# Two attentions of a two-block decoder layer: the values' product taken by turns of two heads, and the chunk mask moved out of TensorE

## The chip, the cores and the metric

One core of a Trainium2 chip runs the whole kernel. The metric is the device time of one execution in microseconds (us); a program of one core has one span, that of its engines from the first instruction to the last. The engines are TensorE (PE in the profile, its weight loads PEld), VectorE (DVE), ScalarE (ACT), GpSimd (POOL) and SyncE (SP), which issues the DMAs.

## The reference

Two blocks follow each other on a sequence of 1024 positions and 1024 features. The first block runs a gated delta rule and a stick-breaking attention beside each other and merges them. The second runs two softmax attentions, MLA and a differential one, then a feed-forward part. Three attentions are concerned here; cut down to them the reference is:

```python
# stick-breaking: 8 heads of 64, causal, blocks of 128 queries
a = where(mask, exp(log_sigmoid(z) + rest), 0)          # z = q k^T * scale, rest: a reversed cumulative sum
o = einsum('bhqk,bhkd->bhqd', a, v)
# MLA: 8 heads, keys of 96 features, values of 64
allowed = (k_idx // 64) <= (q_idx // 64)
probs = softmax(where(allowed, q k^T * scale, -1e30))
o = einsum('bhqk,bhkd->bhqd', probs, v)
# differential: 4 heads, two maps each, bias from a table by distance
logits = where(allowed, q k^T * scale + bias, -1e30)
attn = softmax(logits[0]) - lam * softmax(logits[1])
o = einsum('bhqk,bhkd->bhqd', attn, v)
```

`allowed` is the chunk mask: a query sees all keys of its own chunk of 64 and of the chunks before. Within a tile of 128 queries (two chunks) that hides the tile's second chunk of keys from the tile's first 64 queries.

## The kernel before, in words

All matrix products are float32. An input of a large product is split into a high and a low part, and `mm3` (L250 to L254) multiplies high by high, high by low and low by high. The attention's other products (transposes, the values' product) are plain float32.

**Order of the work.** The kernel is written for one core in a framework that takes the instructions in program order as priorities, plans them against one another, and gives each engine its own order from that; each engine then runs its order strictly. So a product that is written later can stand between two that are written earlier, where the plan saw the second wait. `attend` (L782) drives an attention over a list of items: at step n it calls `s0` of item n (scores and softmax) and `s1` of item n-2 (transpose and values' product), with a `yield` after each. At a `yield`, `mix` steps a second generator, the fill: independent projections, in proportion to the items done. Stick-breaking (`sb`, L823) has the gate projections as fill, with a pool of two PSUM banks for them and one bank (`PT`) for transposes; `mla` (L1169) has the rest of `diff_proj`, and after it the next stage's `out2a`; `diff` has `out2a` and `ple_proj`. `mla_proj`, the stage before `mla`, has five and three banks and most of `diff_proj` as its fill.

**Items.** `pairs` (L885) lists four pairs of heads (p), each over eight tiles of 128 queries (i). For i below 4 an item holds both heads of the pair; from i = 4 on each head is an item of its own. A head at tile i has i + 1 blocks of 128 keys.

**Values' product, before.** `attend_pv` (L889) transposes up to four blocks of an item into the one `pt` bank (L903), copies them to `aT` (L904), does so again for the next four, and then multiplies all blocks, first head first (L907): the weights are 128 x 64 values, so head 0 writes rows 0 to 63 of `po` and head 1 rows 64 to 127. In the trace each float32 product is two records. A transpose uses all 128 columns of the array, the values' product 64.

**Chunk mask, before.** In `mla` and in `diff` a fourth product, in bfloat16, adds -1e30 to the last 64 keys of the last block (L1201, L1304), with the constant `negch`; it closes the group of products of each score tile.

**Around them.** `mla` reads its queries and keys from DRAM (`dr_mla`, 96 feature rows, high and low part; L1171), to which `mla_proj` wrote them with `l_st` (L1127). `diff` loads for each head a `strip` of bias (L1276) that `L1307` adds to the scores while it takes their maximum. `qk_stack` (L719) writes the differential queries and keys to DRAM through tiles `qb_st`, two buffers, evacuated by ACT (L301) and DVE (L302), two tiles behind each other for each half.

Of the kernel before, what the change touches and what calls it, by code (L numbers as in the profile page):

```python
# [75 lines left out]
    return np.ascontiguousarray(onehot), np.ascontiguousarray(rope.reshape(8, 128, 2, 32).transpose(1, 0, 2, 3))  # L76


def layout(inputs):
    a = {k: np.asarray(v) for k, v in inputs.items()}  # L80
    o = {}
# [49 lines left out]
    o["lam"] = np.ascontiguousarray(np.stack([a[f"lambda_{n}_2"][0] for n in ("q1", "k1", "q2", "k2")]))  # L131
    o["rel"] = np.ascontiguousarray(a["rel_bias_2"])
    o["onehot"], o["rope"] = _tables()
    return o


# [15 lines left out]
class Kern:  # L152
# [38 lines left out]
    def consts(self):  # L191
        nc, d, const = self.nc, self.d, self.const
        self.vec = {}
        self.later = []

        def load(n, shape, src):
            t = const.tile(shape, F32, name=n)
            self.vec[n] = t
            return lambda: nc.sync.dma_start(t, src)
        for n in ("b_gate", "cw1", "g_dn", "g_ql", "g_kvl", "g_do", "cw2", "cb2"):  # L200
            self.later.append(load(n, list(d[n].shape), d[n]))
        for n, w in (("a_log", 4), ("dt_bias", 4), ("g_sq", 64), ("g_sk", 64), ("g_dq", 64), ("g_dk", 64), ("g_mq", 96), ("g_mk", 96)):
# [12 lines left out]

        self.negch = const.tile([128, 64], BF16, name="negch")
        nc.gpsimd.memset(self.negch, 0.0)
        nc.gpsimd.memset(self.negch[0:64, :], NEG)
        self.ones = const.tile([128, 128], F32, name="ones")
        nc.gpsimd.memset(self.ones, 1.0)  # L220

        def casts():
            nc.vector.tensor_copy(self.identb, self.ident)
            nc.vector.tensor_copy(self.negub, negu)
        self.later.append(casts)
# [491 lines left out]
    def qk_stack(self, pool, xn, ws, gains, dst):  # L717
# [23 lines left out]
        def stack(gi, half, raw):  # L741
            for pr in range(2):
                p = 2 * (gi % 2) + pr
                st = pool.tile([128, 2, 512], F32R, tag="qb_st", name="qb_st", bufs=2)
                pt = self.PT()
                for j in range(4):
                    nc.tensor.transpose(pt[:, j, :], raw[:, j, pr * 128:pr * 128 + 128], self.ident)
                self.split_evac(st[:, 0], st[:, 1], pt.rearrange("p a b -> p (a b)"))
                a = 2 * (gi // 2)
                nc.sync.dma_start(dst[p, :, a:a + 2, half * 512:half * 512 + 512], st.bitcast(F32))  # L750
                yield
# [70 lines left out]
    def sb(self):  # L822
# [14 lines left out]
        def s0(p, i, hs):  # L837
# [28 lines left out]
            cs = new("cs", 4)  # L866
# [4 lines left out]
            st[p, i, hs] = cs  # L871

        def s1(p, i, hs):
            cs = st.pop((p, i, hs))
            qk, v, ob = st[p]
            po = self.attend_pv(sp, po_, st, cs, v, i, hs, nc.vector.tensor_copy, nc.vector.tensor_copy)
            if hs[-1] == 1:
                nc.vector.tensor_copy(ob[:, i * 128:i * 128 + 128], po)
                if i == NT - 1:
                    nc.sync.dma_start(self.dr_oa[1, :, p, :], ob)  # L880

        yield from self.attend(self.pairs(), s0, s1)
        es.close()
# [2 lines left out]

        return [(p, i, hs) for p in range(4) for i in range(NT) for hs in ([(0, 1)] if i < 4 else [(0,), (1,)])]

    def attend_pv(self, sp, po_, st, e, v, i, hs, *copy):  # L889

        nc = self.nc
        mm = nc.tensor.matmul
        if hs[0] == 0:
            st["po"] = po_.tile([128, 128], F32, tag="po", name="po")
        po = st["po"]
        blocks = [(a, j) for a in range(len(hs)) for j in range(i + 1)]
        aT = sp.tile([128, 8, 128], F32, tag="aT", name="aT", bufs=2)
        step = 4 if i != 2 else 3
        for b0 in range(0, len(blocks), step):
            pt = self.PT()  # L900
            bs = blocks[b0:b0 + step]
            for b, (a, j) in enumerate(bs):
                nc.tensor.transpose(pt[:, b, :], e[:, a, j * 128:j * 128 + 128], self.ident)  # L903
            copy[b0 > 0](aT[:, b0:b0 + len(bs), :], pt[:, :len(bs), :])  # L904
        for b, (a, j) in enumerate(blocks):
            h = hs[a]
            mm(po[64 * h:64 * h + 64, :], v[:, j, h * 64:h * 64 + 64], aT[:, b, :], start=j == 0, stop=j == i)  # L907
        return po

    def merge_in(self):  # L910
# [78 lines left out]
    def layer2(self):  # L989
        nc, d, tc, vec = self.nc, self.d, self.tc, self.vec  # L990
        dr = lambda n, s: self.dram.tile(s, F32, name=n)
        self.dr_mla = dr("dr_mla", [8, 96, 4, 1024])
        self.dr_mv = dr("dr_mv", [128, NT, 512])
        self.dr_dqk = dr("dr_dqk", [4, 128, 4, 1024])
        self.dr_dv = dr("dr_dv", [128, NT, 512])
# [27 lines left out]

    def mla_proj(self):
        nc, d, tc, vec, lp = self.nc, self.d, self.tc, self.vec, self.lp
        rope = lp.tile([128, NT, 2, 32], F32, name="rope")
        nc.sync.dma_start(rope, d["rope"])
        qlT = [self.pair(lp, f"qlT{h}", 2) for h in range(2)]
# [90 lines left out]
        def fin(raw, hg, half, part):  # L1119

            for h in range(4):
# [5 lines left out]
                nc.sync.dma_start(self.dr_mla[4 * hg + h, :, part:part + 2, half * 512:half * 512 + 512], st.bitcast(F32))  # L1127

        units = []
        w = {}  # L1130
# [27 lines left out]

    def mla(self):
        nc, d, tc = self.nc, self.d, self.tc  # L1160
        mm = nc.tensor.matmul
# [5 lines left out]

        def load(p, hh, c, half):

            t = sp.tile([96, 2, 512], F32R, tag=f"qk{c}{half}{hh}", name="qk", bufs=1 + (hh == 1 and c == 1 and half == 0))  # L1170
# [10 lines left out]
        def s0(p, i, hs):  # L1181
# [10 lines left out]
            for a, h in enumerate(hs):  # L1192
                qk = st[p][0]
                qt = qk[h, 0, i // 4]
                for c0 in range(0, nk, 512):
                    n = min(512, nk - c0)
                    last = c0 + n == nk
                    kt = qk[h, 1, c0 // 512]
                    self.mm3(z[:, a, c0:c0 + n], [qt[:, 0, q], qt[:, 1, q]], [kt[:, 0, :n], kt[:, 1, :n]], True, not last)
                    if last:  # L1200
                        mm(z[:, a, nk - 64:nk], self.identb, self.negch, start=False, stop=True)  # L1201
            zz = z[:, :, :nk]
            nm, s, r = (self.small.tile([128, 2], F32, tag=f"a_{n}", name=f"a_{n}", bufs=4)[:, :len(hs)] for n in "msr")
            nc.vector.reduce_max(nm, zz, axis=AX.X, negate=True)
            e = sp.tile([128, 1024], F32, tag="e", name="e", bufs=3)[:, :len(hs) * nk].rearrange("p (a k) -> p a k", a=len(hs))
# [5 lines left out]
            st[p, i, hs] = e  # L1211

        def s1(p, i, hs):
            e = st.pop((p, i, hs))
            qks, v = st[p]
            po = self.attend_pv(sp, po_, st, e, v, i, hs, nc.scalar.copy, nc.vector.tensor_copy)
            if hs[-1] == 1:
                if i % 4 == 0:
                    st["ob"] = sp.tile([128, 512], F32, tag="ob", name="ob", bufs=1)
                nc.vector.tensor_copy(st["ob"][:, i % 4 * 128:i % 4 * 128 + 128], po)  # L1220
                if i % 4 == 3:
                    nc.sync.dma_start(self.dr_mix[:, p, (i - 3) * 128:(i + 1) * 128], st["ob"])

        yield from self.attend(self.pairs(), s0, s1)
        es.close()
# [13 lines left out]
    def diff(self):  # L1239
# [30 lines left out]
        def first(hd):  # L1270
# [3 lines left out]
            skew = self.dr_f[hd][0:1, 127:128]  # L1274
            strip[hd] = qp.tile([128, 1024], F32, tag="strip", name="strip", bufs=2)
            nc.sync.dma_start(strip[hd], bass.AP(tensor=skew.tensor, offset=skew.offset, ap=[[1152, 128], [1, 1024]]))  # L1276
            st[hd] = qk, v, o, sp.tile([128, NT], F32, tag="o_ss", name="o_ss", bufs=2)

        def s0(hd, i):
# [13 lines left out]
            for m in range(2):  # L1293
# [2 lines left out]
                z = zs[:, m if i < 4 else 0]  # L1296
                for c0 in range(0, nk, 512):
                    n = min(512, nk - c0)
                    last = c0 + n == nk
                    kt = qk[c0 // 512][1]  # L1300
                    mm(z[:, c0:c0 + n], qt[:, 0, m, q], kt[:, m, :n], start=True, stop=False)
                    mm(z[:, c0:c0 + n], qt[:, 1, m, q], kt[:, m, :n], start=False, stop=not last)
                    if last:
                        mm(z[:, nk - 64:nk], self.identb, self.negch, start=False, stop=True)  # L1304
                e = sp.tile([128, 1024], F32, tag=f"e{m}", name="e", bufs=(3, 2)[m])[:, :nk]
                mx = self.small.tile([128, 1], F32, tag="a_nm", name="a_nm", bufs=4)
                nc.vector.tensor_tensor_reduce(e, z[:, :nk], strip[hd][:, 896 - 128 * i:1024], 1.0, -3.0e38, ALU.add, ALU.max, mx)  # L1307
# [367 lines left out]
```

## Time and profile before

| | |
|---|---|
| runs shown | 2704.09, 2707.13, 2709.62 us; median 2707.13 us |
| profiled execution | 2711.15 us, of which the span is 2709.3 us |
| busy share of the span | PE 94%, PEld 80%, DVE 54%, ACT 32%, POOL 39% |
| mean granted clock of TensorE | 0.982 |

The profile shows one execution. The profiled execution's own time is 1.85 us longer than its span and 4.0 us over the median of the runs shown. Busy times of an engine are unions of its instructions; matmuls are pipelined, so what a product costs is read from the start of one to the start of the next.

### The profile page before, as it was taken

The page shows a single profiled execution, that of the slowest core. Times are in us where ns is not written, and L with a number is a line of the kernel's source. Part 1 is how long each engine was busy: PE and PEld are TensorE (multiplying, and loading weights), DVE is VectorE, ACT ScalarE, POOL GpSimd, SP SyncE. Part 2 cuts the span into 40 slices and gives each one's busy share as a digit, 9 for nine tenths or more (in the row PEclk, how much of TensorE's full clock was granted, in tenths as well). Part 3 has the DMA queues.
Part 4 walks back from the last instruction along what each step waited for, and adds up shares of the span by engine and source line. Part 5 has one row for each costly group of instructions (what it writes and reads, how often), then busy time and mean ns, then how long its engine had stood idle before and what let it go on. Part 6 is the DMA issues. An engine that isn't in the chain of part 4 may idle for free.

```text
span 2709.3 us, 38990 instructions
## 1 busy us (share of the span) xinstructions
PE 2548.5 (94%) x15298; PEld 2173.9 (80%) x15298; DVE 1461.3 (54%) x2837; ACT 864.7 (32%) x1575; POOL 1057.1 (39%) x920
## 2 busy tenths in 40 slices
PE   6998999999999989999889998889999999999999
PEld 6888888877777768989777787788777777777789
DVE  6565565275666554457844336666454454534372
ACT  3322222154444342122324335463333333201031
POOL 2533332122122234544533232223677777634322
PEclk9999999999999999999989999999999999999999
DMA  4433223153421355322674337554122222523222
GB/s 155 132 103 107 79 86 101 56 142 97 119 86 63 133 175 190 105 82 82 207 200 128 94 123 171 170 186 156 55 79 70 86 85 64 196 83 109 70 82 90
DMA packets 152335, 311.46 MB, mean 115 GB/s; under 512 B 14132, under 2 KB 57396, under 8 KB 152152
## 3 DMA queue, kind: packets, MB, share of 16 engines
q1 hardware_dynamic: 152152, 308.97, 36.7%
q8 instruction: 121, 1.98, 0.3%
q14 instruction: 62, 0.51, 0.1%
HBM read 211.91 MB, written 99.37 MB: 115 GB/s over the span
## 4 chain that ended last, share of the span: by engine, by line
PE 61%; DVE 10%; DMA 5%; ACT 3%; issue 2%; POOL 1%; SPq 0%; ACTq 0%; DVEq 0%; POOLq 0%
PE pj L1525 15%; PE pj L254 10%; PE pj L253 10%; PE pj L252 10%; PE po L907 5%; PE pt L903 3%; DMA dr_mla<-l_st 1%; PE po L1333 1%; PE z L253 1%; DVE cs L868 1%; PE z L252 1%; DMA m_o<-dr_oa 1%; DVE rs_a L293 1%; PE z L254 1%; DVE rs_a L292 1%
## 5 line engine op out<-in xcount | busy, mean ns | idle before, releaser
L243 POOL TENSOR_SCALAR hl<-raw 128x512 fp32r<-128x512 f32 (+3 forms) x270 | 197.6, 737 | 961.0 <-PE pj L254 949.5
L244 POOL TENSOR_TENSOR hl<-raw,hl 128x512 fp32r<-128x512 f32 (+3 forms) x270 | 368.7, 1371 | 16.0
L252 PE MATMUL pj<-hl,xn_0h 128*128 128x256 f32 (+2 forms) x544 | 160.6, 296 | 2.3 <-DVE qb_st L302 1.1
L253 PE MATMUL pj<-hl,xn_0h 128*128 128x256 f32 (+2 forms) x544 | 160.6, 295 | 1.7 <-POOL hl L244 1.7
L252 PE MATMUL pj<-hl,xn_1h 128*128 128x256 f32 (+2 forms) x544 | 159.2, 293 | 0.0
L254 PE MATMUL pj<-hl,xn_1l 128*128 128x256 f32 (+2 forms) x544 | 158.8, 292 | 0.0
L254 PE MATMUL pj<-hl,xn_0l 128*128 128x256 f32 (+2 forms) x544 | 158.7, 292 | 0.0
L253 PE MATMUL pj<-hl,xn_1h 128*128 128x256 f32 (+2 forms) x544 | 158.3, 291 | 0.0
L1506 POOL TENSOR_TENSOR hl<-w_s,hl 128x512 fp32r<-128x512 f32 x88 | 120.9, 1375 | 84.1 <-ACT hl L1505 84.0
L907 PE MATMUL po<-aT,v 128*64 128x128 f32 x1152 | 150.4, 280 | 2.2 <-DVE aT L904 1.6
L254 PE MATMUL pj<-hl,f_hl 128*128 128x512 f32 x352 | 140.4, 401 | 2.9 <-DVE f_hl L1607 2.9
L252 PE MATMUL pj<-hl,f_hh 128*128 128x512 f32 x352 | 140.0, 398 | 2.9 <-DVE xres L1616 2.4
L907 PEld LDWEIGHTS po<-aT,v 128*64 128x64 f32 x1152 | 116.5, 136 | 30.6 <-issue 19.2
L253 PE MATMUL pj<-hl,f_hh 128*128 128x512 f32 x352 | 138.3, 393 | 0.0
L1616 DVE TENSOR_TENSOR xres<-xres,pj 128x512 f32<-128x512 f32 x96 | 65.1, 685 | 126.2 <-PE pj L254 113.2
L1506 POOL TENSOR_TENSOR hl<-raw,hl 128x512 fp32r<-128x512 f32 x66 | 100.2, 1524 | 70.4 <-ACT hl L1505 69.7
L904 DVE COPY aT<-pt 128x512 f32<-128x512 f32 (+3 forms) x128 | 72.5, 566 | 99.2 <-PE pt L903 99.0
L1561 DVE TENSOR_TENSOR f_u<-pj,w_u 128x512 f32<-128x512 f32 x44 | 30.4, 692 | 169.1 <-ACT w_u L1529 96.3
L252 PE MATMUL pj<-xn_0h,hl 128*128 128x512 f32 x288 | 116.8, 406 | 0.0
L252 PE MATMUL pj<-xn_1h,hl 128*128 128x512 f32 x288 | 115.7, 402 | 0.0
L254 PE MATMUL pj<-xn_1h,hl 128*128 128x512 f32 x288 | 114.9, 399 | 0.0
L253 PE MATMUL pj<-xn_1l,hl 128*128 128x512 f32 x288 | 114.8, 399 | 0.0
(599 smaller groups left out, 7436.8 us busy)
## 6 DMA issues: line engine op xcount, KB each, us to landing
raw<-in_w_o_dram SPq DMA_DIRECT2D x28, 512.0 KB, 4.3
dr_mla<-l_st SPq DMA_DIRECT2D x32, 384.0 KB, 3.7
qk<-dr_mla SPq DMA_DIRECT2D x32, 384.0 KB, 4.8
raw<-in_w_fg_dram SPq DMA_DIRECT2D x22, 512.0 KB, 4.5
raw<-in_w_fu_dram SPq DMA_DIRECT2D x22, 512.0 KB, 3.5
dr_h<-f_y SPq DMA_DIRECT2D x22, 512.0 KB, 5.3
raw<-in_w_fd_dram SPq DMA_DIRECT2D x22, 512.0 KB, 3.8
f_y<-dr_h SPq DMA_DIRECT2D x22, 512.0 KB, 4.2
```

The source lines that it names most:

```text
L243: nc.gpsimd.tensor_scalar(hl[:, 0], raw[:, k:k + c], 1.0, 1.0, ALU.mult, ALU.mult)
L244: nc.gpsimd.tensor_tensor(hl[:, 1], raw[:, k:k + c], hl[:, 0].bitcast(F32), ALU.subtract)
L252: mm(ps, lh[0], rh[0], start=first, stop=False)
L253: mm(ps, lh[0], rh[1], start=False, stop=False)
L254: mm(ps, lh[1], rh[0], start=False, stop=last)
L903: nc.tensor.transpose(pt[:, b, :], e[:, a, j * 128:j * 128 + 128], self.ident)
L904: copy[b0 > 0](aT[:, b0:b0 + len(bs), :], pt[:, :len(bs), :])
L907: mm(po[64 * h:64 * h + 64, :], v[:, j, h * 64:h * 64 + 64], aT[:, b, :], start=j == 0, stop=j == i)
L1506: nc.gpsimd.tensor_tensor(hl[:, 1], v, hl[:, 0].bitcast(F32), ALU.subtract)
L1525: nc.tensor.matmul(ps, w[k][l], b[r][:, k, :], start=first and k + n == 0, stop=k == 3 and n == 2, skip_group_check=not first)
L1561: nc.vector.tensor_tensor(u, ps, v, ALU.add)
L1616: nc.vector.tensor_tensor(xr, xr, ps, ALU.add)
```

## The change

It does six things.

1. `attend_pv` no longer works an item at a time. `s1` does nothing for the first head of a split tile; with the second head it takes both. For each two blocks of keys it transposes the two heads' blocks by turns (four transposes, or two at the end of an odd count), copies them, and multiplies them by turns of the heads. `aT` becomes tiles of four blocks, five buffers in `sb` and four in `mla`.
2. The first head's probabilities live longer: `cs` gets five buffers for four, `e` of `mla` four for three.
3. In `mla` the mask's product goes. `dr_mla` has eight more feature rows: for queries row r holds 1 where the position is in chunk 2r, for keys -2^100 where it is in chunk 2r + 1, the low parts 0. Eight DMAs of 128 KB each from an input array write them at the head of `mla_proj`. Query and key tiles have 104 rows.
4. In `diff` the mask's product goes. Behind each strip's load GpSimd writes -1e30 into 64 x 64 of it.
5. `negch` and its two memsets go.
6. `qb_st` has one buffer for two where `qk_stack` runs for the differential attention.

```diff
+    h = np.zeros((NT, 4, T), np.float32)
+    h[:, 0] = chunk == 2 * r
+    h[:, 2] = (chunk == 2 * r + 1) * np.float32(-2.0 ** 100)
...
-                st = pool.tile([128, 2, 512], F32R, tag="qb_st", name="qb_st", bufs=2)
+                st = pool.tile([128, 2, 512], F32R, tag="qb_st", name="qb_st", bufs=1 if pool is getattr(self, "fp", None) else 2)
...
         def s1(p, i, hs):
-            cs = st.pop((p, i, hs))
+            if hs == (0,):
+                return
             qk, v, ob = st[p]
-            po = self.attend_pv(sp, po_, st, cs, v, i, hs, nc.vector.tensor_copy, nc.vector.tensor_copy)
...
+            po = self.attend_pv(sp, po_, st, v, p, i, 5, nc.vector.tensor_copy, nc.vector.tensor_copy)
...
-    def attend_pv(self, sp, po_, st, e, v, i, hs, *copy):
+    def attend_pv(self, sp, po_, st, v, p, i, bufs, *copy):
...
-        blocks = [(a, j) for a in range(len(hs)) for j in range(i + 1)]
-        aT = sp.tile([128, 8, 128], F32, tag="aT", name="aT", bufs=2)
-        step = 4 if i != 2 else 3
-        for b0 in range(0, len(blocks), step):
+        if i < 4:
+            both = st.pop((p, i, (0, 1)))
+            e = [both[:, a] for a in range(2)]
+        else:
+            e = [st.pop((p, i, (a,)))[:, 0] for a in range(2)]
+        po = po_.tile([128, 128], F32, tag="po", name="po")
+        for j0 in range(0, i + 1, 2):
+            blocks = [(j, a) for j in range(j0, min(j0 + 2, i + 1)) for a in range(2)]
+            n = len(blocks)
             pt = self.PT()
...
+            for b, (j, a) in enumerate(blocks):
+                nc.tensor.transpose(pt[:, b, :], e[a][:, j * 128:j * 128 + 128], self.ident)
+            aT = sp.tile([128, 4, 128], F32, tag="aT", name="aT", bufs=bufs)
+            copy[j0 > 0](aT[:, :n], pt[:, :n])
+            for b, (j, a) in enumerate(blocks):
+                nc.tensor.matmul(po[64 * a:64 * a + 64, :], v[:, j, a * 64:a * 64 + 64], aT[:, b, :], start=j == 0, stop=j == i)
...
-        self.dr_mla = dr("dr_mla", [8, 96, 4, 1024])
+        self.dr_mla = dr("dr_mla", [8, 96 + NT, 4, 1024])
...
+        for h in range(8):
+            nc.sync.dma_start(self.dr_mla[h, 96:96 + NT], d["hide"])
...
-                    if last:
-                        mm(z[:, a, nk - 64:nk], self.identb, self.negch, start=False, stop=True)
+                    self.mm3(z[:, a, c0:c0 + n], [qt[:, 0, q], qt[:, 1, q]], [kt[:, 0, :n], kt[:, 1, :n]], True, True)
...
+            nc.gpsimd.memset(strip[hd][0:64, 960:1024], NEG)
...
-                    if last:
-                        mm(z[:, nk - 64:nk], self.identb, self.negch, start=False, stop=True)
+                    mm(z[:, c0:c0 + n], qt[:, 1, m, q], kt[:, m, :n], start=False, stop=True)
```

## Rows read from the trace of the kernel before

**Rows 1.** The page: busy times, PE's slices, granted clock.
```profile
PE 2548.5 (94%) x15298; PEld 2173.9 (80%) x15298; DVE 1461.3 (54%) x2837; ACT 864.7 (32%) x1575; POOL 1057.1 (39%) x920
PE   6998999999999989999889998889999999999999
PEclk9999999999999999999989999999999999999999
```

**Rows 2.** Busy time by stretch: stick-breaking, `mla_proj`, MLA, differential attention.
```profile
core 0: us, PE busy (x) PEld busy (x) DVE busy (x) ACT busy (x) POOL busy (x), PEclk, DMA share, GB/s
540.00:975.00 435.00, 423.67 (x2251) 328.33 (x2249) 271.47 (x333) 187.84 (x246) 103.64 (x96) 1.00 0.39 114
1215.00:1410.00 195.00, 168.04 (x1251) 160.79 (x1250) 141.38 (x371) 55.57 (x116) 88.38 (x73) 0.95 0.53 162
1410.00:1628.00 218.00, 215.22 (x1515) 173.49 (x1515) 86.69 (x179) 84.72 (x191) 63.82 (x82) 0.99 0.39 119
1628.00:1820.00 192.00, 165.24 (x1198) 145.59 (x1196) 129.76 (x412) 105.63 (x290) 46.83 (x44) 0.96 0.63 175
```

**Rows 3.** The instructions of L907, the values' product.
```profile
L907 PE MATMUL po<-aT,v x1152: 272/273/324, 555.9 to 1625.0; 128*64 128x128 f32 x192
```

**Rows 4.** PE in order of time: start, length; both heads of tiles 0 and 1.
```profile
555.35 0.39 PE L253 MATMUL pj<-xn_1l,hl 128*128 128x512 f32 x1
555.58 0.40 PE L254 MATMUL pj<-xn_1h,hl 128*128 128x512 f32 x1
555.91 0.44 PE L907 MATMUL po<-aT,v 128*64 128x128 f32 x4
556.28 0.50 PE L252 MATMUL pj<-xn_1h,hl 128*128 128x512 f32 x1
...
559.90 0.66 PE L907 MATMUL po<-aT,v 128*64 128x128 f32 x8
560.50 0.50 PE L254 MATMUL pj<-xn_1h,hl 128*128 128x512 f32 x1
560.83 0.40 PE L252 MATMUL pj<-xn_1h,hl 128*128 128x512 f32 x1
```

**Rows 5.** The same of one head; the last row is the last stretch.
```profile
616.04 1.09 PE L907 MATMUL po<-aT,v 128*64 128x128 f32 x8
617.06 0.50 PE L253 MATMUL pj<-xn_0l,hl 128*128 128x512 f32 x1
617.39 0.40 PE L254 MATMUL pj<-xn_0h,hl 128*128 128x512 f32 x1
617.63 0.39 PE L252 MATMUL pj<-xn_0h,hl 128*128 128x512 f32 x1
617.95 0.87 PE L907 MATMUL po<-aT,v 128*64 128x128 f32 x6
618.75 0.66 PE L903 MATMUL pt<-cst,cs 128*128 128x128 f32 x4
...
1624.20 1.09 PE L907 MATMUL po<-aT,v 128*64 128x128 f32 x8
```

**Rows 6.** The copies (L904), and what L903 and L907 waited for (us, times).
```profile
L904 DVE COPY aT<-pt x128: 279/609/692, 555.4 to 1622.3; 128x512 f32<-128x512 f32 x64, 128x384 f32<-128x384 f32 x28, 128x256 f32<-128x256 f32 x20, 128x128 f32<-128x128 f32 x16
L904 ACT COPY aT<-pt x48: 372/585/591, 1417.8 to 1620.9; 128x512 f32<-128x512 f32 x40, 128x256 f32<-128x256 f32 x4, 128x384 f32<-128x384 f32 x4
...
  DVE aT L904: 15.5, 34
  ACT aT L904: 7.6, 28
...
  DVE aT L904: 5.9, 10
```

**Rows 7.** PE at the end of stick-breaking: a copy that nothing covers.
```profile
910.14 0.60 PE L903 MATMUL pt<-cst,cs 128*128 128x128 f32 x4
911.52 0.65 PE L903 MATMUL pt<-cst,cs 128*128 128x128 f32 x4 [0.79 <-DVE aT L904]
```

**Rows 8.** PE in MLA around one product of the mask.
```profile
1453.98 0.28 PE L253 MATMUL z<-qk 96*128 96x256 f32 x1
1454.11 0.28 PE L254 MATMUL z<-qk 96*128 96x256 f32 x1
1454.23 0.20 PE L1201 MATMUL z<-negch,identb 128*128 128x64 bf16 x1
1454.27 0.36 PE L252 MATMUL z<-qk 96*128 96x256 f32 x1
1454.47 0.28 PE L253 MATMUL z<-qk 96*128 96x256 f32 x1
```

**Rows 9.** `mla_proj`: DMA times to landing, a wait, ACT's pair, the chain's load.
```profile
dr_dqk<-qb_st SPq DMA_DIRECT2D x12, 512.0 KB, 4.7
...
ACT l_st L301 <- DMA dr_mla<-l_st: 28.9, 14, 5.5
...
1284.77 1.07 ACT L301 CAST qb_st<-pt 128x512 fp32r<-128x512 f32 x2
...
1396.72 12.24 DMA qk<-dr_mla
```

**Rows 10.** The strip's load to its landing, and the mask constant's memset.
```profile
strip<-dr_f SPq DMA_DIRECT2D x4, 512.0 KB, 8.2
...
1.43 0.14 POOL L218 MEMSET negch<- 64x64 bf16 x1
```

More of the change, by code (lines that the diff above doesn't have):

```diff
@@ L76, in _tables, with _hide @@
     return np.ascontiguousarray(onehot), np.ascontiguousarray(rope.reshape(8, 128, 2, 32).transpose(1, 0, 2, 3))
+def _hide():
+    chunk = np.arange(T) // 64
+    r = np.arange(NT)[:, None]
+    h = np.zeros((NT, 4, T), np.float32)
+    h[:, 0] = chunk == 2 * r
+    h[:, 2] = (chunk == 2 * r + 1) * np.float32(-2.0 ** 100)
+    return h
 def layout(inputs):
@@ L133, in layout @@
     o["onehot"], o["rope"] = _tables()
+    o["hide"] = _hide()
     return o
@@ L214, in consts @@
         nc.gpsimd.affine_select(self.negsb, self.negsb, [[-1, 128]], ALU.is_gt, NEG, base=0, channel_multiplier=1)
-        self.negch = const.tile([128, 64], BF16, name="negch")
-        nc.gpsimd.memset(self.negch, 0.0)
-        nc.gpsimd.memset(self.negch[0:64, :], NEG)
         self.ones = const.tile([128, 128], F32, name="ones")
@@ L865, in s0 @@
             nc.vector.scalar_tensor_tensor(e, zz, 0.0, e, ALU.max, ALU.add)
-            cs = new("cs", 4)
+            cs = new("cs", 5)
             for a in range(len(hs)):
@@ L873, in s1 @@
         def s1(p, i, hs):
-            cs = st.pop((p, i, hs))
+            if hs == (0,):
+                return
             qk, v, ob = st[p]
-            po = self.attend_pv(sp, po_, st, cs, v, i, hs, nc.vector.tensor_copy, nc.vector.tensor_copy)
[L877 to L880, printed above, removed]
+            po = self.attend_pv(sp, po_, st, v, p, i, 5, nc.vector.tensor_copy, nc.vector.tensor_copy)
+            nc.vector.tensor_copy(ob[:, i * 128:i * 128 + 128], po)
+            if i == NT - 1:
+                nc.sync.dma_start(self.dr_oa[1, :, p, :], ob)
         yield from self.attend(self.pairs(), s0, s1)
@@ L887, in pairs @@
         return [(p, i, hs) for p in range(4) for i in range(NT) for hs in ([(0, 1)] if i < 4 else [(0,), (1,)])]
-    def attend_pv(self, sp, po_, st, e, v, i, hs, *copy):
+    def attend_pv(self, sp, po_, st, v, p, i, bufs, *copy):
         nc = self.nc
[L892 to L895, printed above, removed]
-        blocks = [(a, j) for a in range(len(hs)) for j in range(i + 1)]
-        aT = sp.tile([128, 8, 128], F32, tag="aT", name="aT", bufs=2)
-        step = 4 if i != 2 else 3
-        for b0 in range(0, len(blocks), step):
-            pt = self.PT()
[L901 to L907, printed above, removed]
+        if i < 4:
[7 more added lines that the diff above has]
+            n = len(blocks)
+            pt = self.PT()
+            for b, (j, a) in enumerate(blocks):
[4 more added lines that the diff above has]
+                nc.tensor.matmul(po[64 * a:64 * a + 64, :], v[:, j, a * 64:a * 64 + 64], aT[:, b, :], start=j == 0, stop=j == i)
         return po
@@ L1126, in fin @@
                 self.split_evac(st[:, 0], st[:, 1], pt[:96].rearrange("p a b -> p (a b)"))
-                nc.sync.dma_start(self.dr_mla[4 * hg + h, :, part:part + 2, half * 512:half * 512 + 512], st.bitcast(F32))
+                nc.sync.dma_start(self.dr_mla[4 * hg + h, 0:96, part:part + 2, half * 512:half * 512 + 512], st.bitcast(F32))
         units = []
@@ L1168, in load @@
         def load(p, hh, c, half):
-            t = sp.tile([96, 2, 512], F32R, tag=f"qk{c}{half}{hh}", name="qk", bufs=1 + (hh == 1 and c == 1 and half == 0))
+            t = sp.tile([96 + NT, 2, 512], F32R, tag=f"qk{c}{half}{hh}", name="qk", bufs=1 + (hh == 1 and c == 1 and half == 0))
             nc.sync.dma_start(t.bitcast(F32), self.dr_mla[2 * p + hh][:, 2 * c:2 * c + 2, half * 512:half * 512 + 512])
@@ L1196, in s0 @@
                     n = min(512, nk - c0)
-                    last = c0 + n == nk
                     kt = qk[h, 1, c0 // 512]
-                    self.mm3(z[:, a, c0:c0 + n], [qt[:, 0, q], qt[:, 1, q]], [kt[:, 0, :n], kt[:, 1, :n]], True, not last)
-                    if last:
-                        mm(z[:, a, nk - 64:nk], self.identb, self.negch, start=False, stop=True)
+                    self.mm3(z[:, a, c0:c0 + n], [qt[:, 0, q], qt[:, 1, q]], [kt[:, 0, :n], kt[:, 1, :n]], True, True)
             zz = z[:, :, :nk]
@@ L1204, in s0 @@
             nc.vector.reduce_max(nm, zz, axis=AX.X, negate=True)
-            e = sp.tile([128, 1024], F32, tag="e", name="e", bufs=3)[:, :len(hs) * nk].rearrange("p (a k) -> p a k", a=len(hs))
+            e = sp.tile([128, 1024], F32, tag="e", name="e", bufs=4)[:, :len(hs) * nk].rearrange("p (a k) -> p a k", a=len(hs))
             for a in range(len(hs)):
@@ L1213, in s1 @@
         def s1(p, i, hs):
-            e = st.pop((p, i, hs))
+            if hs == (0,):
+                return
             qks, v = st[p]
[L1216 to L1222, printed above, removed]
+            po = self.attend_pv(sp, po_, st, v, p, i, 4, nc.scalar.copy, nc.vector.tensor_copy)
+            if i % 4 == 0:
+                st["ob"] = sp.tile([128, 512], F32, tag="ob", name="ob", bufs=1)
+            nc.vector.tensor_copy(st["ob"][:, i % 4 * 128:i % 4 * 128 + 128], po)
+            if i % 4 == 3:
+                nc.sync.dma_start(self.dr_mix[:, p, (i - 3) * 128:(i + 1) * 128], st["ob"])
         yield from self.attend(self.pairs(), s0, s1)
@@ L1298, in s0 @@
                     n = min(512, nk - c0)
-                    last = c0 + n == nk
                     kt = qk[c0 // 512][1]
                     mm(z[:, c0:c0 + n], qt[:, 0, m, q], kt[:, m, :n], start=True, stop=False)
-                    mm(z[:, c0:c0 + n], qt[:, 1, m, q], kt[:, m, :n], start=False, stop=not last)
-                    if last:
-                        mm(z[:, nk - 64:nk], self.identb, self.negch, start=False, stop=True)
+                    mm(z[:, c0:c0 + n], qt[:, 1, m, q], kt[:, m, :n], start=False, stop=True)
                 e = sp.tile([128, 1024], F32, tag=f"e{m}", name="e", bufs=(3, 2)[m])[:, :nk]
```

1 line of the change is left out of this document (removed).

## The prediction, made before the changed kernel was run

> **What bounds the kernel now.** I read the page first: PE is busy 94% of the span, its slices are eights and nines, and its clock is granted nearly in full [rows 1]. Then the busy times by stretch, since the change lies in three attentions and the stage between them [rows 2]. Stick-breaking has PE busy 424 of 435 us and MLA 215 of 218, with no other engine over two thirds: in these two a microsecond of PE is a microsecond of time. The differential attention has 165 of 192, `mla_proj` 168 of 195; there PE also waits, and only a part of what PE saves comes out. Then the values' product: 1152 records, all of 64 columns, each shown with some 273 ns [rows 3]. That length is a pipelined one, so I read prices from starts instead.
>
> **Price of the values' product.** One head: from 616.04 to the next start, 617.06, eight records take 1.02 us, and six take 0.80 (617.95 to 618.75) [rows 5]. That is 0.11 us a record and 0.14 us once for a stretch. Around a stretch more is lost: the 512-column product ahead of it takes 0.33 or 0.32 us to the next start for 0.23 or 0.24 among its like, say 0.09 more, and the one behind it 0.33, 0.10 more [rows 4, 5]. So a stretch of 64-column products between 128-column ones costs 0.14 + 0.19 = 0.33 us over its records. The timeline has 140 such stretches, 71 in stick-breaking and 69 in MLA, the first at 555.91 and the last at 1624.20 [rows 4, 5].
>
> The trace also shows what two heads do together. At tiles 0 and 1 both heads stand in one stretch: four records take 0.37 us to the next start, eight take 0.60 [rows 4]. One head would need 0.58 and 1.02. The two halves of the array's columns work side by side, and a pair of records costs one 0.11. Tile 0 is the changed order itself, one block of each head.
>
> The Trainium skill, TensorE: Matmul & The Clock Gate, Part 3 (The mechanism), says that a weight load overlaps running matmuls only where the row group differs, and that matmuls start and end in strict order. The two heads differ in columns and not in rows, so by it turns of heads would overlap nothing and the sum of this part would be +12 us in place of -49. The eight records in 0.60 us speak against it; what it would do is the third rival.
>
> **Part 1, turns of heads.** Before: 1152 x 0.11 = 126.7 us, less 48 records that already overlap at tiles 0 and 1 (six for each of eight head pairs in the two attentions, 5.3), plus 140 x 0.33 = 46.2: 167.6 us. After: a head pair has 1+1+2+2+3+3+4+4 = 20 groups, 16 of eight records and 4 of four. If every group is a stretch of its own, 128 x (0.60 + 0.19) + 32 x (0.37 + 0.19) = 119.0 us. Difference **-48.6**, half in each attention. Twenty stretches more are counted in it. Were some groups to run together, each join would save 0.33; twenty joins give 7 more, kept for the lower end. Transposes are as many as before.
>
> What is hidden: the copies. There are 176 now [rows 6] and 160 after. Between four transposes and the products that need them lie a copy of 0.6 to 0.7 us and two hand-overs; today fill or scores usually stand there in PE's order, and PE waits 29 us in all for these copies [rows 6]. An uncovered one costs 0.79 us [rows 7]. Today the products of the first four blocks also cover the second copy; after the change each group's products wait right behind their own copy. Between nothing and 160 x 0.79 - 29 = 97 us more I take **+5**: stick-breaking and MLA have fill throughout, and the plan has put it into nearly every such gap.
>
> The first head's step in `s1` is empty now and the second's double. At the end of each attention the last four groups follow each other, copy by copy, where two single-head halves were spread over two steps: at most four uncovered copies each, 2 x 3.2 us; there is fill at both ends, so **+2**. The extra buffers of `cs` and `e` are what lets the first head's wait; with them nothing waits longer. A full `cs` would hold VectorE's scan and behind it the copies.
>
> **Part 2, the mask's products.** Each of MLA's 64 takes 0.04 us to the next start (1454.23 to 1454.27), and the score product behind it takes 0.20 where its like takes 0.12 [rows 8]: 0.12 us, 64 times, **-7.7** in MLA, where PE is the bound. The differential attention has 64 more of the same form, another 7.7 on PE. As PE idles there for 27 of 192 us [rows 2], between 0 and 7.7 comes out; I take half, **-3.8**.
>
> **Part 3, what comes in.** Query and key tiles have 104 rows for 96. A score product of 96 rows and 256 columns takes 0.12 to 0.13 us to the next start [rows 8], half of what 512 columns take with 128 rows, 0.23 [rows 4], so eight more rows cost PE nothing; the load at MLA's entry, 12.24 us in the chain [rows 9], grows by at most 8%: **+1**; the later loads lie a whole head pair ahead. The eight DMAs of the mask rows, 1 MB from DRAM to DRAM, stand on SP's queue ahead of the rope table and whatever `mla_proj` issues behind. Issue and transfer lie beside the first projections, while DMA is busy half of that stage [rows 2]. Without cover they cost about what one 512 KB load takes to its landing, 8 us [rows 10]; I take **+1**.
>
> The four memsets on POOL cost about 0.14 us each [rows 10], but each waits there for its strip, 8.2 us from issue [rows 10], and the weight splits of the fill queue behind. POOL is busy for a quarter of that stage [rows 2]. Bounds 0 and 4 x 8.2; taken **+1**, since the next head's strip is loaded half a head ahead. Behind the memset stand the additions of the bias on VectorE, which wait for that load already. The two memsets of `negch` that go are worth nothing.
>
> One `qb_st` buffer: in `mla_proj` twelve tiles are evacuated and sent, mostly two right behind each other, as at 1284.77 [rows 9]. The second must now wait 4.7 us for the first to land [rows 9], and in ACT's strict order whatever stands behind it waits too; PE waits next, for transpose banks. ACT already loses 28.9 us in 14 waits of this kind for `l_st` [rows 9] without being the bound. Six pairs at 4.7 us give at most 28, cover gives 0; the plan can move other work ahead, so **+6**.
>
> **Sum.** -48.6 + 5 + 2 - 7.7 - 3.8 + 1 + 1 + 1 + 6 = **-44.1 us**. Against the profiled execution's 2711.15 us that is 2667. The runs shown have their median 4.0 us lower, at 2707.13, so the number for the runs is **2663**.
>
> **Rivals.**
> - *MLA runs short of cover* (faster, but less). MLA has 80 of the groups, in 218 us, and its own scores and the rest of `diff_proj` to lay between. For: after the change PE has 32 us less of work there, while the groups need as many gaps filled. Against: near MLA's end the plan already fetches products of the following stage. With half of the groups uncovered, 40 x 0.79 = 32, of which some 10 are in today's waits and in the +5: +22, **2685**.
> - *The copies take the bound* (slower). One mechanism everywhere: transposes, copy, products and the next transposes through the one `pt` bank follow each other, and the plan puts nothing between. Without the waits the sum is -49.1, so it decides from (49 + 29) / 0.79 = 99 uncovered groups of 160. With three quarters uncovered, 120 x 0.79 - 29 = +66 in place of +5: **2724**. Against: PE's order today.
> - *The change doesn't do what it says* (slower). Turns of heads overlap nothing, as when an engine takes its products and weights strictly in order. Then part 1 costs 128 x 1.21 + 32 x 0.77 = 179.5 us, +11.9 in place of -48.6, and the time is 2663 + 60.5 = **2724**. Against: rows 4, where tile 0 is this order.
>
> **How the numbers follow.** A measurement of this kernel can tell about 0.2% from no change, 5.4 us. Forecast 0.82, MLA short of cover 0.09, copies the bound 0.05, no overlap 0.04. Faster: the forecast and nearly all of the first rival, 0.90. Same: what lies near the turning point of the first two rivals, 0.03. Slower: 0.07. The range's lower end has every term at its better bound (-48.6 - 7.7 - 7.7 = -64, 2643) and twenty joined stretches, 2637. Its upper end takes the forecast with `qb_st` at its bound (+22), which gives 2685, and 13 more for copies and memsets, which also holds the first rival: 2698.
>
> **What the changed profile would show.** Stretches of eight records of the values' product in about 0.66 us, near 160 of them, at 0.60 us to the next start: right. Eight in 1.09: the third rival. PE's waits for `aT` at 30 to 40 us: right; near 100: the second. MLA's 218 us should shrink by about 30, stick-breaking by about 22. ACT's wait on the DMA of `qb_st` should be new, and `mla_proj` a few us longer. No rows of a 64-column mask product. Most of the doubt lies in how the plan orders PE: if it doesn't lay fill behind the transposes, the forecast is wrong.

## The result and the profile after

The changed kernel takes 2673.79 us in the median (2666.2 to 2674.78, four runs), the kernel before beside it 2708.38: a ratio of 0.9858 [0.9843, 0.9872], some 38 us less. Run again beside other executions of the kernel before it came to 0.9843 [0.9822, 0.9863]. The forecast was 2663 in a range of 2637 to 2698. The profiled execution took 2666.2 us with a span of 2664.3, 45 less than the profiled one before.

The page after; its rows answer to [rows 1].

```profile
PE 2486.0 (93%) x15170; PEld 2114.7 (79%) x15170; DVE 1467.1 (55%) x2837; ACT 856.4 (32%) x1559; POOL 1060.1 (40%) x922
PE   6998999999999999999889969899999999999999
PEclk9999999999999999999989999999999999999999
```

PE is busy 62.5 us less, but the span is only 45 shorter: in the 24th of the 40 slices a six has come in. To see where it lies I cut both traces at the same events. The views below are busy times by stretch: stick-breaking up to the last values' product, `mla_proj`, MLA from its first score to its last store, the 25 us behind that, and the rest of the differential attention up to its last score product. First the kernel before:

```profile
core 0: us, PE busy (x) PEld busy (x) DVE busy (x) ACT busy (x) POOL busy (x), PEclk, DMA share, GB/s
536.20:914.10 377.90, 371.31 (x2032) 287.18 (x2030) 243.30 (x298) 166.55 (x212) 84.73 (x80) 1.00 0.35 99
1169.40:1392.10 222.70, 198.71 (x1383) 190.41 (x1384) 164.50 (x459) 66.91 (x141) 99.92 (x84) 0.95 0.42 133
1409.10:1625.60 216.50, 213.72 (x1498) 171.99 (x1499) 85.93 (x177) 84.72 (x191) 62.42 (x80) 0.98 0.40 119
1625.60:1650.60 25.00, 22.29 (x174) 21.75 (x174) 7.44 (x24) 2.23 (x8) 13.57 (x15) 0.93 0.79 186
1650.60:1799.80 149.20, 126.35 (x889) 107.92 (x888) 108.60 (x357) 89.09 (x250) 31.30 (x28) 0.97 0.62 173
```

The same cuts after the change:

```profile
536.10:900.40 364.30, 345.60 (x2032) 257.28 (x2030) 241.03 (x290) 166.92 (x212) 85.39 (x80) 1.00 0.36 104
1148.80:1371.20 222.40, 197.93 (x1382) 189.24 (x1383) 162.59 (x459) 67.12 (x141) 99.93 (x84) 0.96 0.42 134
1387.20:1574.50 187.30, 174.77 (x1397) 136.01 (x1397) 90.32 (x181) 72.91 (x171) 62.35 (x80) 0.99 0.45 135
1574.50:1599.50 25.00, 9.24 (x23) 6.04 (x23) 7.68 (x44) 6.18 (x22) 0.14 (x1) 0.54 0.95 218
1599.50:1753.90 154.40, 141.77 (x1008) 129.42 (x1009) 112.41 (x341) 88.22 (x238) 46.23 (x44) 0.96 0.61 172
```

In stick-breaking PE does the same 2032 instructions in 25.7 us less, of which 13.6 come out of the stretch; another 6.9 come out of its merge behind (255.3 to 248.4). MLA is 29.2 shorter, `mla_proj` as long as before. The differential attention, 174.2 before, takes 179.4: right behind MLA PE has 9.24 us of work in 25 where it had 22.29, at a granted clock of 0.54, close to the lower of its two levels (1.2 of 2.4 GHz).

PE in order of time in stick-breaking after, the answer to [rows 4]:

```profile
841.42 0.39 PE L261 MATMUL pj<-xn_0l,hl 128*128 128x512 f32 x1
841.74 0.66 PE L916 MATMUL po<-aT,v 128*64 128x128 f32 x8
842.33 0.50 PE L262 MATMUL pj<-xn_0h,hl 128*128 128x512 f32 x1
842.66 0.39 PE L260 MATMUL pj<-xn_0h,hl 128*128 128x512 f32 x1
```

Eight records of two heads take 0.59 us to the next start, where one head took 1.02 [rows 5]. The 512-column products around them still take 0.32 and 0.33.

### The profile page after: what moved, and what is told of

It is laid out like the page before. It is cut to its first block, busy times and chain, and to the rows that moved or that the text cites. A ratio compares the mean times of both kernels' runs of the same rounds, so it can differ in the third digit from the quotient of the medians.

```text
span 2664.3 us, 38694 instructions
## 1 busy us (share of the span) xinstructions
PE 2486.0 (93%) x15170; PEld 2114.7 (79%) x15170; DVE 1467.1 (55%) x2837; ACT 856.4 (32%) x1559; POOL 1060.1 (40%) x922
## 4 chain that ended last, share of the span: by engine, by line
PE 54%; DVE 13%; DMA 5%; ACT 4%; issue 4%; POOL 1%; SPq 0%; ACTq 0%; DVEq 0%; POOLq 0%
PE pj L1531 15%; PE pj L262 9%; PE pj L261 9%; PE pj L260 9%; PE po L916 3%; PE pt L912 2%; DVE cs L876 2%; DVE e L873 1%; DMA m_o<-dr_oa 1%; PE po L1339 1%; DVE aT L914 1%; DVE cs L877 1%; DMA dr_dqk<-qb_st 1%; DMA dr_mla<-l_st 1%; DVE rs_a L300 1%
## 5 line engine op out<-in xcount | busy, mean ns | idle before, releaser
L252 POOL TENSOR_TENSOR hl<-raw,hl 128x512 fp32r<-128x512 f32 (+3 forms) x270 | 372.3, 1385 | 16.1
L914 DVE COPY aT<-pt 128x512 f32<-128x512 f32 (+1 forms) x128 | 80.5, 629 | 102.6 <-PE pt L912 101.7
L916 PE MATMUL po<-aT,v 128*64 128x128 f32 x1152 | 98.2, 287 | 26.1 <-DVE aT L914 21.1
L916 PEld LDWEIGHTS po<-aT,v 128*64 128x64 f32 x1152 | 59.8, 136 | 73.2 <-DVE aT L914 53.3
L260 PE MATMUL pj<-xn_0h,hl 128*128 128x512 f32 x288 | 116.9, 406 | 0.0
L262 PE MATMUL pj<-xn_0h,hl 128*128 128x512 f32 x288 | 115.1, 400 | 0.0
```

What stands on the lines that cost most here:

```text
L252: nc.gpsimd.tensor_tensor(hl[:, 1], raw[:, k:k + c], hl[:, 0].bitcast(F32), ALU.subtract)
L260: mm(ps, lh[0], rh[0], start=first, stop=False)
L262: mm(ps, lh[1], rh[0], start=False, stop=last)
L914: copy[j0 > 0](aT[:, :n], pt[:, :n])
L916: nc.tensor.matmul(po[64 * a:64 * a + 64, :], v[:, j, a * 64:a * 64 + 64], aT[:, b, :], start=j == 0, stop=j == i)
```

## Experiments

The ratios are against the kernel before on the same chip; labels up to `e4` shared one chip, `e5` to `e8` a second, `e9` to `e11` a third.

**One part alone.** `e1` is the changed kernel with the mask's products put back (points 3 to 5 of the change undone).

```diff
...
-            t = sp.tile([96 + NT, 2, 512], F32R, tag=f"qk{c}{half}{hh}", ...
+            t = sp.tile([96, 2, 512], F32R, tag=f"qk{c}{half}{hh}", ...
...
+                    if c0 + n == nk:
+                        nc.tensor.matmul(z[:, a, nk - 64:nk], self.identb, self.negch, start=False, stop=True)
...
-            nc.gpsimd.memset(strip[hd][0:64, 960:1024], NEG)
```

> The changed kernel with the mask's products back in both attentions (dr_mla 96 rows, no memset on the strip): turns of heads and their buffers alone. Theory (the two parts add up; MLA is bound by PE): MLA's stretch is 7 us longer than in the changed kernel, the differential attention 0 to 5 longer, stick-breaking the same; some 10 us slower than the changed kernel, 22 to 28 faster than before. The 8 records of the values' product take 0.59 us to the next start in 160 stretches. Rival (the mask's removal carries the gain): within 8 us of before.

Measured: 2684.34 us, 0.9912 [0.9895, 0.9929], 24 us less than before. The turns alone bring most of it, and by the ratios the masks' part in the whole is about 15 us. By stage it is 10.1 us: in `e1` MLA and the differential attention take 376.8 us together, in the changed kernel 366.7. The two traces differ by another 6.7 us in the first 540 us, where PE has the same instructions. The rows of `e1`:

```profile
1394.00:1586.10 192.10, 181.59 (x1461) 139.65 (x1461) 90.37 (x181) 72.64 (x171) 62.12 (x80) 0.98 0.43 127
1586.10:1770.80 184.70, 154.21 (x1095) 135.58 (x1096) 121.92 (x385) 94.14 (x260) 46.32 (x41) 0.92 0.64 174
```

`e2` is the complement: the kernel before with points 3 to 5.

> The kernel before with the mask's products moved into feature rows and strip, nothing else. Theory: 64 products of 0.12 us off a stretch that PE bounds, MLA 7 us shorter; the differential attention, where PE waits anyway, 0 to 5; 8 to 12 us faster than before in all. Rival (the memset's wait on POOL and the larger loads eat it): within 4 us of before, with POOL's waits for the strip near 8 us each.

Measured: 2710.64 against 2710.60, 1.0001 [0.9991, 1.0010]. Without the turns the masks' part is worth nothing that can be seen. Two further kernels take it apart: `e6` has the mask rows of MLA alone, `e7` the mask in the strip of the differential attention alone.

> The kernel before with the mask moved into feature rows in MLA alone; the differential attention keeps its products. Theory (64 products of 0.12 us off a stretch that PE bounds): MLA's stretch 6 to 8 us shorter and the kernel 4 to 8 us faster. Rival (work that MLA no longer does in time has to be done in the next stage, or the larger loads eat it): MLA shorter by some 6 us in the trace, the kernel within 3 us of before.

> The kernel before with the mask moved into the strip in the differential attention alone; MLA keeps its products. Theory (PE is not the bound there, and the memset's wait costs little): within 4 us of before. Rival (the memset holds POOL until each strip has landed, the weight splits behind it come late): 3 to 8 us slower, with POOL's wait ahead of the memset in the trace and PE waiting for weights behind it.

Measured: `e6` 1.0004 [0.9992, 1.0016], `e7` 0.9979 [0.9968, 0.9990], 5.7 us less and more than I had expected. The waits of `e7` in the differential attention show the one that the prediction priced:

```profile
POOL strip L1277 <- DMA strip<-dr_f: 48.8, 4, 23.1
```

POOL stands for 48.8 us, in four waits, and the kernel is faster all the same. In `e2` the busy times of MLA and of the differential attention are these:

```profile
1414.30:1625.90 211.60, 208.08 (x1434) 168.53 (x1435) 85.51 (x177) 85.50 (x191) 62.38 (x80) 0.99 0.42 127
1625.90:1799.50 173.60, 146.30 (x998) 128.99 (x997) 114.47 (x380) 91.56 (x256) 45.38 (x45) 0.95 0.65 176
```

MLA has its 64 instructions less (1434 for 1498) and PE 5.6 us less work there, and MLA is 4.9 us shorter, where the prediction priced 7.7: 0.09 us a product and not 0.12. The two stages together take 390.7 us before, 389.2 in `e6`, 385.3 in `e7` and 385.2 in `e2`. For `e7` that agrees with its median. In `e6` MLA is 2.4 us shorter, not 6 to 8, and the differential attention 0.9 longer. So the two parts don't add up in `e2`, and what its trace gains isn't in its median. Why is open.

**Do the two heads overlap, and does the order matter?** `e3` writes both heads to the same 64 columns of the array, side by side in the free dimension of `po`, by the same turns; what is computed is unchanged, and a tile has one more copy.

```diff
-        po = po_.tile([128, 128], F32, tag="po", name="po")
+        po = po_.tile([64, 2, 128], F32, tag="po", name="po")
...
-                nc.tensor.matmul(po[64 * a:64 * a + 64, :], v[:, j, a * 64:a * 64 + 64], aT[:, b, :], start=j == 0, stop=j == i)
+                nc.tensor.matmul(po[0:64, a], v[:, j, a * 64:a * 64 + 64], aT[:, b, :], start=j == 0 and a == 0, stop=j == i, skip_group_check=True)
...
```

> The changed kernel with both heads' products written to rows 0 to 63 of the output, side by side in its free dimension, and one more VectorE copy of 0.3 us for each tile: the same groups and stretches, but both heads in the same columns of the array. Theory (the gain is the two column halves working together): eight records take 1.02 us to the next start in place of 0.59, 128 x 0.43 + 32 x 0.21 = 62 us more PE work, 50 to 62 us slower than the changed kernel, so 15 to 28 slower than before. Rival (the gain comes from smaller groups and better cover, not from the columns): within 15 us of the changed kernel.

Measured: 2735.29 us, 1.0094 [1.0079, 1.0110]: slower than before, and some 65 us slower than the changed kernel. PE in order of time:

```profile
879.76 0.39 PE L261 MATMUL pj<-xn_1l,hl 128*128 128x512 f32 x1
880.08 1.09 PE L917 MATMUL po<-aT,v 128*64 128x128 f32 x8
881.10 0.44 PE L913 MATMUL pt<-cst,cs 128*128 128x128 f32 x2
```

Eight records take 1.02 us to the next start again. The gain is the overlap of the two halves of the columns. `e8` keeps both halves, but in a group of blocks gives first the one head's products, then the other's:

```diff
-            for b, (j, a) in enumerate(blocks):
+            for b, (j, a) in sorted(enumerate(blocks), key=lambda x: (x[1][1], x[1][0])):
```

> The changed kernel with the products of a group in the order of the kernel before, first head's two blocks, then the second's. Transposes, copies and groups stay. Theory (PE lets the two column halves run side by side whenever both heads stand in one stretch, as tile 1 of the kernel before showed): eight records still take 0.59 to 0.60 us to the next start, and the time is within 4 us of the changed kernel. Rival (the turn of heads in the order is what makes them overlap): 0.8 to 1.02 us, 25 to 60 us slower than the changed kernel.

Measured: 2672.70 us, 0.9855 [0.9836, 0.9875], as the changed kernel beside it (0.9843). In order of time:

```profile
850.59 0.40 PE L261 MATMUL pj<-xn_0l,hl 128*128 128x512 f32 x1
850.92 0.66 PE L916 MATMUL po<-aT,v 128*64 128x128 f32 x8
851.51 0.50 PE L262 MATMUL pj<-xn_0h,hl 128*128 128x512 f32 x1
```

Still 0.59 us: what counts is that both heads are in the stretch; turns within it are not needed. This gain has now been seen in [rows 4], in the changed kernel and here, and taken away by `e3` alone.

**The hole behind MLA.** The changed kernel's PE at the end of MLA, with its idle times in brackets:

```profile
1573.47 0.66 PE L916 MATMUL po<-aT,v 128*64 128x128 f32 x8 [0.78 <-DVE aT L914]
...
1584.65 0.77 PE L1309 MATMUL z<-k,q 128*128 128x128 f32 x2 [10.52 <-DMA q<-dr_dqk]
...
1587.05 0.77 PE L1310 MATMUL z<-k,q 128*128 128x128 f32 x2 [1.63 <-DMA q<-dr_dqk]
```

PE waits 10.5 us for the first loads of the differential attention. In the kernel before, the output projection's products fill this place; their input `m_o` is loaded ahead of MLA's last store on SP's queue. First that kernel, then the changed one:

```profile
1593.38 0.91 SPq L1363 DMA_DIRECT2D m_o<-dr_mix  x2
...
1603.10 15.21 SPq L1363 DMA_DIRECT2D m_o<-dr_mix  x4
1625.64 0.32 SPq L1222 DMA_DIRECT2D dr_mix<-ob  x1
```

```profile
1574.49 0.32 SPq L1229 DMA_DIRECT2D dr_mix<-ob  x1
...
1576.99 0.61 SPq L779 DMA_DIRECT2D k<-dr_dqk  x1
...
1587.62 2.11 SPq L1369 DMA_DIRECT2D m_o<-dr_mix  x2
```

My theory: MLA's pool is larger, by the buffer of `e`, and `m_o`, which before lay beside it, must now wait for the pool's end. `e4` gives the room back, 4 KB a partition, with two `aT` buffers in MLA for four:

```diff
-            po = self.attend_pv(sp, po_, st, v, p, i, 4, nc.scalar.copy, nc.vector.tensor_copy)
+            po = self.attend_pv(sp, po_, st, v, p, i, 2, nc.scalar.copy, nc.vector.tensor_copy)
```

> The changed kernel with two aT buffers in MLA in place of four, 4 KB less in its pool, the size by which the fourth buffer of e made it larger. Theory (the entry into the differential attention lost its cover because the loads of the next stage's fill, m_o, lie where MLA's enlarged pool lies and wait for its end): m_o is loaded ahead of MLA's last tile again, PE is busy over 80% of the 25 us behind MLA in place of 39%, and the kernel is 8 to 12 us faster than the changed one. Rival (the loads are late for another cause, or PE's idle there is made up for later): within 3 us of the changed kernel. Second rival (aT needs its four buffers): MLA's stretch grows by over 5 us.

Measured: 2668.11 us, 0.9842 [0.9826, 0.9858], some 4 us less than the changed kernel by the ratios, not the 8 to 12 that I had expected. In its trace `m_o` is loaded ahead of the last store again, and the 25 us behind MLA are filled:

```profile
1585.50:1610.50 25.00, 21.29 (x156) 20.10 (x154) 9.92 (x27) 2.83 (x9) 12.22 (x14) 0.93 0.92 212
```

The differential attention takes 170.0 us for 179.4, but MLA 191.3 for 187.3, since the fill now lies there (294 of its products for 229). To size what is left I ran the changed kernel and `e4` again, as `e5` and `e11`:

> The changed kernel once more, beside runs of before on the same chip, as the measure for the others of this call. Theory (turns of heads and the mask add up): 33 to 40 us faster than before, and its stretch from the end of mla_proj to the end of the differential attention near 406 us, as in the first profile. Rival (the first comparison lay at one edge of the noise): 22 to 30 us faster, no more than the turns alone.

> The room experiment once more, now in five rounds, since the first left open whether it differs from the changed kernel (0.9842 against 0.9858 and 0.9843). Theory (cover behind MLA is worth part of PE's idle there): 3 to 8 us faster than the changed kernel's 0.985, so 0.982 to 0.984. Rival (MLA takes up the fill and becomes longer by as much): 0.985 within 0.001.

Measured: `e5` 0.9843 [0.9822, 0.9863], some 43 us and a little more than expected, and `e11` 0.9833 [0.9818, 0.9848]. By itself the room is worth some 3 us, and the intervals overlap.

The other traces bear the theory out. A buffer of `e` takes 4 KB a partition. Where `aT` and `e` of MLA hold 20 KB (8 and 12 in the kernel before, `e2`, `e6` and `e7`; 4 and 16 in `e4`, `e9` and `e11`), the first load of `m_o` is issued 25 to 32 us ahead of MLA's last store, and PE is busy for 20.4 to 24.5 of the 25 us behind it. Where they hold 24 KB (8 and 16 in the changed kernel, `e1`, `e3`, `e5`, `e8` and `e10`), it is issued 13 us behind that store, and PE is busy for 8.9 to 9.6 us. So the hole goes with the sum, and not with the number of buffers of one kind.

**The waits for the copies.** `e9` takes `e4` and multiplies each group of blocks only after the next group's transposes, so that a copy has those as cover:

```diff
...
+            if pend:
+                values(*pend)
+            pend = aT, blocks
+        values(*pend)
...
```

`values` holds the loop of products, word for word. `e10` is the same with four `aT` buffers.

> The changed kernel with two aT buffers in MLA (as in the room experiment) and each group's products written one group later: transposes and copy of group g, then the products of group g - 1, so that these stand beside the copy. Theory (what the turns of heads cost over the sum's stretches is PE's waits for its own group's copy, 23 us by the rows of waits): these waits fall under 8 us, stick-breaking's stretch (end of the delta rule to the last values' product) from 364 to some 350 us, the kernel 10 to 20 us faster than the changed one. Rival (PE's plan had already laid fill there, so a later place brings nothing, or the transposes wait more): within 5 us of the room experiment.

> The same with MLA's four aT buffers left as in the changed kernel, so without the room for the next stage's loads. Theory (the two effects add): the waits for the copies as low as in the run with two buffers, PE under 50% busy in the 25 us behind MLA, 3 to 8 us slower than the run with two buffers. Rival (cover at the entry only moves work): within 3 us of it.

Measured: `e9` 2653.47 us, **0.9787 [0.9773, 0.9801]**, 58 us less than before and the fastest kernel here; `e10` 2670.64 us, 0.9853 [0.9829, 0.9876]. PE's waits for the copies in stick-breaking, first of the changed kernel, then of `e9`:

```profile
PE po L916 <- DVE aT L914: 15.9, 20, 1.7
```

```profile
PE pt L918 <- DVE aT L920: 7.5, 13, 1.7
PE po L911 <- DVE aT L920: 1.0, 2, 0.8
```

They fall by 7.4 us, and stick-breaking with its merge by 6.6 (612.7 to 606.1). Most of the rest comes from the differential attention (179.4 to 167.2), right behind MLA; the 25 us there, of `e9` and then of `e10`:

```profile
1571.10:1596.10 25.00, 24.49 (x197) 23.64 (x196) 12.54 (x47) 5.94 (x21) 11.47 (x13) 1.00 0.88 195
```

```profile
1586.10:1611.10 25.00, 9.33 (x24) 6.12 (x24) 7.88 (x45) 6.18 (x22) 0.14 (x1) 0.54 0.96 219
```

The hole follows the room again. But the two edits are worth more together than apart: the room alone about 3 us, the later products alone nothing that can be seen (`e10` 0.9853, the changed kernel 0.9843 and 0.9858), both together 15 to 19. Against `e11`, which has the same room and ran beside it, `e9` is 13.6 us faster. I had expected 3 to 8 between `e9` and `e10` and measured 17. The two traces place it: MLA and the differential attention take 355.6 us in `e9` and 372.3 in `e10`, 16.7 more. The other 15.8 by which these two executions differ lie in stages in which both have the same instructions; the one of `e10` was 9.8 above its median, the one of `e9` 5.5 below. Within the 16.7, 12.8 are the hole's stage; the rest is MLA, where `e10` has the 1397 instructions of the changed kernel at a lower clock (187.30 us there, at 0.99):

```profile
1393.80:1586.10 192.30, 182.68 (x1397) 141.46 (x1397) 91.47 (x181) 74.44 (x171) 62.23 (x80) 0.96 0.44 131
```

Why the clock was lower there, and so what the later products are worth in MLA without the room, stays open.

## Why the prediction was right, step by step

**Price of a stretch: right, shown.** After the change there are 80 and 79 stretches (160 forecast), with means of 0.59 us for eight records and 0.37 for four (0.60 and 0.37 forecast). `e3` and `e8` settle the rival that the turns overlap nothing: the overlap is real and doesn't depend on the order. The rule of the Trainium skill, TensorE: Matmul & The Clock Gate, Part 3 (The mechanism), by which weight loads overlap running matmuls only where the row group differs, doesn't decide the time of these products. The two halves differ in columns alone, and 0.59 against 1.02 us shows that they overlap all the same. That the turns would then overlap nothing was the prediction's inference from the rule.

**Copies: mechanism right, size too small.** I took +5. PE's own waits for `aT` were 3.6 and 1.6 us in stick-breaking and 1.1 in MLA, together 6.3; first these rows, then those after:

```profile
PE pt L903 <- DVE aT L904: 3.6, 6, 0.9
PE po L907 <- DVE aT L904: 1.6, 2, 0.8
...
PE pt L903 <- ACT aT L904: 1.1, 3, 0.4
```

```profile
PE po L916 <- DVE aT L914: 15.9, 20, 1.7
...
PE po L916 <- DVE aT L914: 5.2, 8, 0.8
...
PE po L916 <- ACT aT L914: 2.0, 4, 0.7
```

That is 23.1, so +17. The windows agree for stick-breaking: PE idles 18.7 us of it (364.30 less 345.60) where it idled 6.6. The step that failed is that fill would lie in nearly every gap. My measuring rod was also bad: the 29 us of [rows 6] count the weight loads' idle time too, and by the same view it is now 85, near what I had named as the sign of the second rival:

```profile
  DVE aT L914: 74.4, 121
  ACT aT L914: 10.9, 29
```

The time shows that most of this stands beside other PE work. Stick-breaking with its merge came to -20.5, where the working has half of part 1, the copies and the end of one attention, some -21; the merge made up for what the copies took. The prediction has no term for the merge, so this agreement is luck. But the merge's gain repeats: 245.5 to 251.6 us in the eight kernels whose heads overlap, 255.1 to 258.3 in the four without the new order. No run here shows where it comes from.

**MLA: right in the sum, in part by luck.** -29.2, and -1.0 at its entry load, where part 1, the mask and the small terms give some -28. Of the mask's 7.7 some 5 came (`e1` to the changed kernel, 192.1 to 187.3). The first rival, MLA short of cover, shows in 7.2 us of waits, against the 22 that it priced; PE idles 12.5 us there for 2.8. And a part of MLA's work has moved behind it: 37 products of the fill, 4.1 us of PE, as the rows of the instructions on the tile `pj` in MLA show, before and after:

```profile
1409.10:1625.60 216.50, 40.46 (x266) 35.26 (x267) 0.69 (x1) 3.52 (x6) 0.98 0.40 119
```

```profile
1387.20:1574.50 187.30, 36.35 (x229) 31.51 (x229) 0.00 (x0) 3.54 (x6) 0.99 0.45 135
```

Without that move MLA would have become some 25 us shorter, by this estimate.

**Differential attention: wrong.** I took -3.8 for the mask and +1 for the strips, -2.8 in all; the trace has +5.2, of which the fill that comes over from MLA is some 4.5 (PE's work on `pj` goes from 61.89 to 66.41 us there). The strips' wait is harmless (`e7`), and the mask is worth about 5 us there (184.7 in `e1` to 179.4). What I missed is the sentence that with the extra buffers "nothing waits longer": I thought of the tiles in them and not of the room. It delays `m_o`, and with it the fill behind MLA, as `e4` and `e9` show. That sentence is the step that failed here.

**`qb_st`: too dear.** I took +6 between 0 and 28; `mla_proj` went from 222.7 to 222.4. ACT's new wait is there:

```profile
ACT qb_st L309 <- DMA dr_dqk<-qb_st: 5.5, 3, 3.9
```

Three waits and not six, and ACT is no bound there. The eight DMAs of the mask rows, +1, cost nothing that the trace shows. Nothing holds them, and they are issued between 37.8 and 131.3 us, not at `mla_proj`; the first:

```profile
37.81 0.60 SPq L1036 DMA_DIRECT2D dr_mla<-in_hide_dram  x1
```

**The sum.** By the traces -45.0 us, forecast -44.1; in it the copies (12 too cheap) and the differential attention (8 too cheap) stand against `mla_proj` (7 too dear), the merge and MLA. So the total is better than its parts, and that is luck. By the interval of the ratio it is 35 to 43 us, so the forecast of 2663, 44.1 below 2707.13, lies a little too low but well inside its range.

## What to carry to other kernels

When products use half of the array's columns, put the work for both halves into the same stretch, in any order: here a pair then cost what one cost. Then look at what fed them: a copy that earlier products used to cover stands bare, and giving each group's products one group later covers most of it again (PE's waits for the copies were 23.1 us in the changed kernel and 9.4 in `e9`). Before adding buffers to a pool, look at what of the next stage lies beside it: 4 KB a partition that could be spared emptied 13 us of PE behind the attention, and only with that room given back did the later products show in the time.

## What was not expected of the hardware

The first stage, up to the end of the delta rule, in which PE has the same work in all these kernels, ends between 535.7 and 545.8 us in the thirteen profiled executions. The mean granted clock over it is 0.98 or 0.99 in the six that end by 537.3 us, and 0.97 in the seven that end at 540.7 or later. Between 135 and 240 us it was this, in the kernel before and in `e2`:

```profile
135.00:240.00 105.00, 98.04 (x538) 84.74 (x537) 62.31 (x103) 24.11 (x38) 32.93 (x28) 0.97 0.36 115
```

```profile
135.00:240.00 105.00, 98.22 (x519) 84.80 (x518) 61.83 (x101) 23.53 (x37) 33.09 (x29) 0.94 0.35 115
```

The same busy time holds 538 instructions at a clock of 0.97 and 519 at 0.94. What lowers the clock in some executions no run here shows. So effects of a few microseconds were read stage by stage, and from medians where no stage could be cut out.
